# A scan stage on single blocks or on pairs: visits of TensorE, table loads and recurrences

## The chip, the cores and the metric

The kernel runs on one core of a Trainium2 chip. The metric is the device time of one execution in microseconds, lower is better. The core has five engines with queues of their own: TensorE (PE in the profile, its weight loads are PEld), VectorE (DVE), ScalarE (ACT), GpSimd (POOL) and SyncE (SP), which only issues transfers here. They wait for each other by semaphores. Each engine works through its instructions in the order in which they were put into the program.

## The reference

Two layers of a decoder trunk on 256 positions with 2048 channels. The first (state-space scan and attention beside each other) and the closing layer norms are not touched here. The second layer is the one of the change, cut to what matters:

```python
def s5_ssm(u, ...):                      # u: (1, 256, 2048) = 128 groups of 16 channels
    lam_bar = jnp.exp(lam * dt)          # 64 complex states per group
    b_bar = ((lam_bar - 1.0) / lam)[..., None] * (b_re + 1j * b_im)
    bu = jnp.einsum('gnm,blgm->blgn', b_bar, u)      # encode
    hs = scan over l of h = lam_bar * h + bu         # recurrence
    y = jnp.einsum('gmn,blgn->blgm', c_mat, hs).real # decode
    return y + d_skip * u

def s5_mixer(x, ...):
    u, gate = jnp.split(x @ w_in, 2, axis=-1)
    y = gelu(s5_ssm(u, ...))
    ga, gb = jnp.split(y @ w_glu, 2, axis=-1)
    return (ga * sigmoid(gb) * silu(gate)) @ w_out
```

## The kernel before

**The large products.** All weight matrices are streamed once, in units of 512 KB (`raw`, 128 x 1024 floats). For each unit SP loads `raw` (line 227), ACT rounds it to its high part `wh` (L230), and DVE takes the rest `wl` (L232), so that three matmuls of reduced precision give a product of full precision. `split_to` keeps this three units ahead of TensorE, with four buffers each. `wmm` (L297, 24 matmuls of 256 columns a unit) and `xmm` (L276, 12 of 512 columns a unit) are the large matmuls, written to the tiles `main`. `product` runs eight units and after each of them calls `pump`, which hands out the next entries of two lists: `jobs` (work that belongs to the product just done) and `back` (work of a stage in the background, paced by `goal` so that it is spread evenly over the units that are left). So small work is put between the units of the large products. A scheduler then places the instructions of each engine's queue; `tc.issue_after` keeps a job behind a given split in that order.

**The scan stage** is such a background stage. It lies beside the eight products with `wi1` (input projection of the second layer: four products of kind "w" with 256 columns, then four of kind "x" with 512) and the first units of the GLU product. The 128 groups are cut into 16 blocks of 8. For each block `b`, `ssm(b)` gives the steps, and `at(t, f)` files step `f` under the number `t`; all steps, sorted by number, make up `back`. With `t = 2 * b` they are:

- `load` (t - 2): POOL's queue loads the table `wt` (128 x 1792 floats, 896 KB: encode weights, decode weights, and the phase tables `cos` and `sin`) from the scratch `wb`. The tile has four buffers.
- `table` (t - 1): POOL writes the recurrence coefficients `rt`.
- `enc` (t): 16 matmuls of 64 x 64 on the inputs `um` into the tile `enc`. TensorE is used as four quadrants.
- `rec1` (t + 1): DVE turns the result by the phases (four operations of `turned` and two sums, L1159, L1166, L1167).
- `rec2` (t + 2): DVE runs two scans (L1174) into `gt`, turns back (L1161) and combines (L1176, L1177).
- `dec` (t + 4): 24 matmuls of 64 x 64, of which 16 read `gt` (L1190, L1194), into the tile `dec`. It comes in the same step as `enc` of block b + 2, so that one stop of TensorE does both.
- `act` (t + 5): ACT applies GELU into `ys`; after every second block POOL's queue stores it to `yd`.

`u_store` writes the finished columns of `u` to the scratch `ud`; `u_load` (L1115, L1116; four transfers on POOL's queue, for two blocks together) reads them back as `um` in another layout. `y_load` and `y_split` read `yd` back and split it (L1227 on ACT, L1228 on DVE) for the GLU product, which needs the last quarter only in its last two units.

In this text a visit is a stretch in which TensorE leaves the large matmuls for the small ones of `enc` and `dec`.

Of the kernel before, what the change touches and what calls it, by code (L numbers as in the profile page):

```python
# [9 lines left out]
F32 = mybir.dt.float32  # L10
F32R = mybir.dt.float32r
AF = mybir.ActivationFunctionType
# [4 lines left out]
P = 128  # L17
# [145 lines left out]
def trunk(tc, io, out):  # L163
# [4 lines left out]
    def nm(s):  # L168
        count[0] += 1
        return f"{s}_{count[0]}"  # L170

    with ExitStack() as top:
# [917 lines left out]
        with ExitStack() as l1:  # L1090
# [3 lines left out]
            def w1(tag, shape, bufs=2, dt=F32):  # L1094
                return wk.tile(shape, dt, tag=tag, bufs=bufs, name=nm(tag))
# [24 lines left out]
            def at(t, f):  # L1120
                steps.setdefault(t, []).append(f)

            ysd = {}

            def ssm(b):
                j, h, b2 = b // 4, (b // 2) % 2, b % 2
                d = {}
                tiles = [(e, i, i ^ e) for e in range(2) for i in range(2)]

                def load():  # L1130
                    wt = d["w"] = w1("wt", [P, 1792], 4)
                    nc.gpsimd.dma_start(wt, wb[b])
                    ph = wt[:, 1280:1792].rearrange("p (a n) -> p a n", a=2)
                    d["cos"] = ph[:, 0, :].unsqueeze(1).to_broadcast([P, 2, 256])
                    d["sin"] = ph[:, 1, :].unsqueeze(1).to_broadcast([P, 2, 256])

                def table():
                    rt = d["rt"] = w1("rt", [P, 4, 64])
                    G.memset(rt[:, :, 0:1], 0.0)
                    G.tensor_copy(rt[:, :, 1:], rho[:, 4 * b : 4 * b + 4].unsqueeze(2).to_broadcast([P, 4, 63]))  # L1140

                def enc():
                    px = d["x"] = sp.tile([P, 2, 512], F32, tag="enc", name=nm("enc"))
                    wt, u = d["w"], um[b // 2]
                    for q in range(2):
                        for r in range(2):
                            for e, i, at in tiles:
                                a = 2 * q + e
                                T.matmul(px[64 * at : 64 * at + 64, i, r * 128 + q * 64 : r * 128 + q * 64 + 64],  # L1149
                                         wt[64 * i : 64 * i + 64, a * P + 64 * r : a * P + 64 * r + 64],  # L1150
                                         u[64 * i : 64 * i + 64, 4 * b2 + a, :], start=True, stop=True)

                def turned(src):
                    p1, p2 = w1("p1", [P, 2, 256]), w1("p2", [P, 2, 256])
                    for p, t in ((p1, d["cos"]), (p2, d["sin"])):
                        if src is None:
                            t4 = t.rearrange("p r (i n) -> p r i n", i=2)
                            sv = d["x"][:, :, 0:256].rearrange("p i (r n) -> p r i n", r=2)
                            V.tensor_tensor(p.rearrange("p r (i n) -> p r i n", i=2), sv, t4, op=OP.mult)  # L1159
                        else:  # L1160
                            V.tensor_tensor(p, src, t, op=OP.mult)  # L1161
                    return p1, p2

                def rec1():
                    p1, p2 = turned(None)
                    V.tensor_tensor(p1[:, 0], p1[:, 0], p2[:, 1], op=OP.add)  # L1166
                    V.tensor_tensor(p1[:, 1], p1[:, 1], p2[:, 0], op=OP.subtract)  # L1167
                    d["p"] = p1

                def rec2():  # L1170
                    rt = d["rt"].rearrange("p a c -> p (a c)")
                    gt = d["g"] = w1("gt", [P, 2, 256])
                    for r in range(2):
                        V.tensor_tensor_scan(gt[:, r, :], rt, d["p"][:, r, :], 0.0, op0=OP.mult, op1=OP.add)  # L1174
                    p1, p2 = turned(gt)
                    V.tensor_tensor(gt[:, 0], p1[:, 0], p2[:, 1], op=OP.subtract)  # L1176
                    V.scalar_tensor_tensor(gt[:, 1], p1[:, 1], -1.0, p2[:, 0], op0=OP.mult, op1=OP.subtract)  # L1177

                def dec():
                    wt, u, gt = d["w"], um[b // 2], d["g"]  # L1180
                    py = d["y"] = sp.tile([P, 2, 512], F32, tag="dec", name=nm("dec"))
                    for q in range(2):
                        for part in range(3):
                            for e, i, at in tiles:
                                a = 2 * q + e
                                rows = slice(64 * at, 64 * at + 64)
                                o = py[64 * e : 64 * e + 64, at, q * 64 : q * 64 + 64]
                                if part == 0:
                                    rhs = u[rows, 8 + 2 * b2 + q, :] if e else u[rows, 4 * b2 + a, :]
                                    T.matmul(o, wt[rows, 1024 + 64 * a : 1088 + 64 * a], rhs, start=True, stop=False)  # L1190
                                else:
                                    k = 512 + 256 * (part - 1) + 64 * (2 * i + q)
                                    n = 64 * (2 * i + q)
                                    T.matmul(o[:, 1:64], wt[rows, k : k + 64], gt[rows, part - 1, n : n + 63], start=False, stop=part == 2)  # L1194

                def act():
                    if b2 == 0:
                        ysd[0] = w1("ys", [P, 2, 4, 64], 1)
                    ys = ysd[0]
                    A.activation(ys[:, :, 2 * b2 : 2 * b2 + 2, :], d["y"][:, :, 0:128].rearrange("p i (q c) -> p i q c", c=64),  # L1200
                                 AF.Gelu_apprx_tanh)
                    if b2 == 1:
                        dst = yd[j][16 * h : 16 * h + 16].rearrange("(i q e) a c -> e a i q c", i=2, e=2)
                        for i in range(2):
                            nc.gpsimd.dma_start(dst[0, :, i], ys[0:64, i])
                            nc.gpsimd.dma_start(dst[1, :, 1 - i], ys[64:128, i])

                t = 2 * b
                at(t + 5, act)
                at(t + 4, dec)  # L1210
                at(t + 2, rec2)
                at(t + 1, rec1)
                at(t, enc)
                at(t - 1, table)
                at(t - 2, load)

            def y_load(j):
                y5[j] = w1("ut", [P, 4, S], 1)
                nc.gpsimd.dma_start(y5[j], yd[j].rearrange("g a c -> (g a c)").rearrange("(f p t) -> p f t", p=P, t=S))
# [7 lines left out]
                A.activation(y5["h"][:, fs, :], yt, AF.Copy)  # L1227
                V.tensor_tensor(y5["l"][:, fs, :], yt, y5["h"][:, fs, :].bitcast(F32), op=OP.subtract)  # L1228
# [116 lines left out]
```

## Time and profile before

| what | value |
|---|---|
| median of 3 runs | 1352.6 us (1352.0 to 1353.1) |
| the profiled execution | 1355.75 us |
| its span | 1353.9 us |
| granted clock of TensorE | 0.996 |
| DMA, mean over the span | 209 GB/s |
| scan stage, first to last small matmul | 911.6 to 1088.2 us |

The profile is of one execution. Its own time is 3.15 us over the median, and its span is 1.85 us shorter than its own time. In the rows below, a time is the start in us from the span's start, and the length of a matmul is longer than the step to the next one, since they overlap. "<-" in brackets names what ended an engine's idle time. Busy shares are means over stages of different kinds, so the rows of the scan stage count, not those of the page alone.

### The profile page before, as it was taken

How to read it: one execution, taken by the hardware profiler on the slowest of the kernel's cores; microseconds unless marked ns; L12 is line 12 of the kernel's file. 1: busy time of each engine (PE TensorE's matmuls, PEld its weight loads, DVE VectorE, ACT ScalarE, POOL GpSimd, SP SyncE). 2: the span in 40 equal slices, each digit the busy share in tenths (PEclk: the TensorE clock that was granted, in tenths of full speed). 3: DMA queues.
4: the chain of work that ended last, by engine and by line, in shares of the span. 5: the costliest groups of instructions: out<-in, count | busy, mean ns of one | idle time of the engine just before them, and what ended most of it. 6: DMA issues, size and time to landing. Idle time of an engine off the chain costs nothing.

```text
span 1353.9 us, 24904 instructions
## 1 busy us (share of the span) xinstructions
PE 1337.0 (99%) x9839; PEld 1205.5 (89%) x9839; DVE 981.2 (72%) x1560; ACT 673.0 (50%) x870; POOL 364.8 (27%) x648
## 2 busy tenths in 40 slices
PE   9999999999999999999999999999999999999996
PEld 8999999998998998998988888899988888888885
DVE  5767856787687879689787766748889856555556
ACT  5566567764544553554554334334444545444441
POOL 0041000122026528616798500022343100000001
PEclk9999999999999999999999999999999999999998
DMA  8655555545546756856767778497989766666762
GB/s 313 192 171 176 173 171 158 157 143 178 175 135 207 254 163 203 269 160 206 232 206 243 232 232 302 136 300 223 318 275 326 217 211 189 187 196 188 250 214 81
DMA packets 80741, 283.01 MB, mean 209 GB/s; under 512 B 9840, under 2 KB 12528, under 8 KB 80112
## 3 DMA queue, kind: packets, MB, share of 16 engines
q1 hardware_dynamic: 68112, 239.33, 56.2%
q0 software_dynamic: 7328, 30.42, 6.5%
q10 hardware_dynamic: 5184, 11.67, 2.3%
q8 instruction: 77, 1.26, 0.4%
q14 instruction: 40, 0.33, 0.1%
HBM read 260.41 MB, written 20.97 MB: 208 GB/s over the span
## 4 chain that ended last, share of the span: by engine, by line
PE 93%; DVE 4%; DMA 2%; issue 1%; ACT 0%; POOL 0%; SPq 0%; POOLq 0%; ACTq 0%; DVEq 0%
PE main L276 43%; PE main L297 42%; DVE wl L232 1%; PE aux L381 1%; PE aux L812 1%; PE aux L719 1%; PE enc L1149 1%; DMA bc<-in_s5bc 1%; PE dec L1194 1%; PE aux L924 1%; PE aux L892 1%; DMA ud<-ut 0%; PE aux L782 0%; PE dec L1190 0%; PE aux L715 0%
## 5 line engine op out<-in xcount | busy, mean ns | idle before, releaser
L232 DVE TENSOR_TENSOR wl<-raw,wh 128x1024 fp32r<-128x1024 f32 x431 | 538.4, 1251 | 323.4 <-ACT wh L230 317.4
L230 ACT ACTIVATE wh<-raw 128x1024 fp32r<-128x1024 f32 x431 | 455.8, 1059 | 580.3 <-PE main L276 269.2
L297 PE MATMUL main<-A,wh 128*128 128x256 f32 x1408 | 400.7, 285 | 1.3 <-ACT wh L230 1.1
L297 PE MATMUL main<-B,wh 128*128 128x256 f32 x1408 | 398.0, 284 | 0.0
L297 PE MATMUL main<-A,wl 128*128 128x256 f32 x1408 | 394.5, 283 | 0.0
L297 PEld LDWEIGHTS main<-A,wh 128*128 128x128 f32 x1408 | 269.7, 192 | 3.0 <-ACT wh L230 1.3
L297 PEld LDWEIGHTS main<-B,wh 128*128 128x128 f32 x1408 | 269.8, 192 | 0.4
L297 PEld LDWEIGHTS main<-A,wl 128*128 128x128 f32 x1408 | 267.8, 192 | 0.2 <-issue 0.2
L276 PE MATMUL main<-wl,A 128*128 128x512 f32 x512 | 200.5, 392 | 0.5 <-DVE wl L232 0.5
L276 PE MATMUL main<-wh,A 128*128 128x512 f32 x512 | 200.5, 392 | 0.0
L276 PE MATMUL main<-wh,B 128*128 128x512 f32 x512 | 199.9, 390 | 0.0
L276 PE MATMUL main<-wh,C 128*128 128x512 f32 x384 | 150.7, 393 | 0.0
L276 PE MATMUL main<-wh,F 128*128 128x512 f32 x384 | 149.8, 390 | 0.0
L276 PE MATMUL main<-wl,C 128*128 128x512 f32 x384 | 149.7, 390 | 0.0
L276 PEld LDWEIGHTS main<-wl,A 128*128 128x128 f32 x512 | 96.2, 188 | 21.3 <-DVE wl L232 1.8
L276 PEld LDWEIGHTS main<-wh,B 128*128 128x128 f32 x512 | 96.2, 188 | 19.9
L276 PEld LDWEIGHTS main<-wh,A 128*128 128x128 f32 x512 | 96.1, 188 | 19.8 <-issue 0.2
L653 POOL TENSOR_TENSOR c<-c 128x8 f32<-128x8 f32 (+2 forms) x192 | 106.7, 574 | 25.5 <-DMA wb<-c 18.0
L276 PEld LDWEIGHTS main<-wh,F 128*128 128x128 f32 x384 | 72.1, 188 | 15.3
L276 PEld LDWEIGHTS main<-wh,C 128*128 128x128 f32 x384 | 72.1, 188 | 15.1
L276 PEld LDWEIGHTS main<-wl,C 128*128 128x128 f32 x384 | 72.1, 188 | 14.6
L873 POOL TENSOR_TENSOR a<-a,b 64x512 f32<-64x512 f32 x16 | 28.2, 1769 | 169.1 <-DVE b L872 132.1
(279 smaller groups left out, 1651.6 us busy)
## 6 DMA issues: line engine op xcount, KB each, us to landing
raw<-in_wi SPq DMA_DIRECT2D x271, 512.0 KB, 4.0
raw<-in_wo SPq DMA_DIRECT2D x96, 512.0 KB, 4.3
raw<-in_wglu SPq DMA_DIRECT2D x64, 512.0 KB, 3.6
wt<-wb POOLq DMA_DIRECT2D x16, 896.0 KB, 6.9
wb<-ob ACTq DMA_DIRECT2D x16, 512.0 KB, 5.8
bc<-in_s5bc SPq DMA_DIRECT2D x16, 256.0 KB, 4.6
wb<-c POOLq DMA_DIRECT2D x16, 256.0 KB, 3.4
wb<-om ACTq DMA_DIRECT2D x16, 128.0 KB, 4.3
```

The lines of the kernel that those rows point to most:

```text
L230: high = A.activation(wh, raw, AF.Copy)
L232: splits[n] = (loaded[-1], high, V.tensor_tensor(wl, raw, wh.bitcast(F32), op=OP.subtract))
L276: T.matmul(ps[o], l[:, k, sl], r[:, j, :], start=start and i == 0, stop=stop and i == 2)
L297: T.matmul(pv[o // 2][:, o % 2, :], l[:, j, sl], r[:, k, :], start=first and i == 0 and o % 2 == 0, stop=end and i == 2 and o % 2 == 1, sk ...
L381: end = T.transpose(dst[:, i * P : i * P + P], s, ident)
L653: G.tensor_tensor(p[:, :, :, 0:m], cs[:, :, :, 1 : m + 1], cs[:, i, :, n : n + 1].unsqueeze(1).to_broadcast([P, 2, 4, m]), op=OP.mult)
L719: T.matmul(pk[at : at + 64, a * 16 : a * 16 + 16], ev[:, a, 64 * i : 64 * i + 64], cv[:, a, i, :], start=True, stop=True)
L812: T.matmul(yo, xs[:, 0, xc], df[:, i, 0:256], start=True, stop=False)
L873: turns.append(G.tensor_tensor(q[0:64], q[0:64], tm, op=OP.add))
L892: T.matmul(px[:, 128:384], qT[:, h, P:S], kT[:, h, :], start=True, stop=True)
L924: T.matmul(po, v[:, 0, hs], pT[:, i, 0:256], start=True, stop=False)
L1149: T.matmul(px[64 * at : 64 * at + 64, i, r * 128 + q * 64 : r * 128 + q * 64 + 64], wt[64 * i : 64 * i + 64, a * P + 64 * r : a * P + 64 * ...
```

## The change

Steps are made for eight pairs of blocks instead of 16 blocks. One table tile holds both blocks of a pair (two buffers of 2 x 1792), filled by two transfers four steps ahead. `enc` makes the 32 matmuls of a pair, `dec` its 48. The recurrences run over both blocks at once: the products from the tile `enc` stay 512 wide and are four, the sums become 512 wide, the two scans 512, the two products behind them 1024, and the combining of `gt` becomes a step of its own, `rec3`, 512 wide. One GELU serves a pair. `rt`, `p1`, `p2` and `gt` have one buffer instead of two; the GLU stage takes its halves of `gt` and `p1` from them. The inputs `um` are loaded three steps ahead of the encode. The core of the diff:

```diff
-            def ssm(b):
-                j, h, b2 = b // 4, (b // 2) % 2, b % 2
+            def ssm(n):
+                j, h = n // 2, n % 2
...
                 def load():
-                    wt = d["w"] = w1("wt", [P, 1792], 4)
-                    nc.gpsimd.dma_start(wt, wb[b])
...
+                    wt = d["w"] = w1("wt", [P, 2, 1792])
+                    for k in range(2):
+                        nc.gpsimd.dma_start(wt[:, k, :], wb[2 * n + k])
+                    d["cos"], d["sin"] = wt[:, :, 1280:1536], wt[:, :, 1536:1792]

                 def table():
-                    rt = d["rt"] = w1("rt", [P, 4, 64])
+                    rt = d["rt"] = w1("rt", [P, 8, 64], 1)
                     G.memset(rt[:, :, 0:1], 0.0)
-                    G.tensor_copy(rt[:, :, 1:], rho[:, 4 * b : 4 * b + 4].unsqueeze(2).to_broadcast([P, 4, 63]))
+                    G.tensor_copy(rt[:, :, 1:], rho[:, 8 * n : 8 * n + 8].unsqueeze(2).to_broadcast([P, 8, 63]))
...
+                def parts():
+                    return w1("p1", [P, 2, 2, 256], 1), w1("p2", [P, 2, 2, 256], 1)

                 def rec1():
-                    p1, p2 = turned(None)
+                    p1, p2 = parts()
+                    for k in range(2):
+                        for p, t in ((p1, "cos"), (p2, "sin")):
...
+                            V.tensor_tensor(p[:, :, k, :].rearrange("p r (i n) -> p r i n", i=2), sv, t4, op=OP.mult)
                     V.tensor_tensor(p1[:, 0], p1[:, 0], p2[:, 1], op=OP.add)
                     V.tensor_tensor(p1[:, 1], p1[:, 1], p2[:, 0], op=OP.subtract)
                     d["p"] = p1

                 def rec2():
                     rt = d["rt"].rearrange("p a c -> p (a c)")
-                    gt = d["g"] = w1("gt", [P, 2, 256])
+                    gt = d["g"] = w1("gt", [P, 2, 2, 256], 1)
                     for r in range(2):
-                        V.tensor_tensor_scan(gt[:, r, :], rt, d["p"][:, r, :], 0.0, op0=OP.mult, op1=OP.add)
-                    p1, p2 = turned(gt)
+                        V.tensor_tensor_scan(gt[:, r].rearrange("p k n -> p (k n)"), rt, d["p"][:, r].rearrange("p k n -> p (k n)"), 0.0, op0=OP.mult, op1=OP.add)
+                    d["q"] = parts()
+                    for p, t in zip(d["q"], ("cos", "sin")):
+                        V.tensor_tensor(p, gt, d[t].unsqueeze(1).to_broadcast([P, 2, 2, 256]), op=OP.mult)
+
+                def rec3():
+                    gt, (p1, p2) = d["g"], d["q"]
                     V.tensor_tensor(gt[:, 0], p1[:, 0], p2[:, 1], op=OP.subtract)
                     V.scalar_tensor_tensor(gt[:, 1], p1[:, 1], -1.0, p2[:, 0], op0=OP.mult, op1=OP.subtract)
...
-                t = 2 * b
+                t = 4 * n
                 at(t + 5, act)
                 at(t + 4, dec)
+                at(t + 3, rec3)
                 at(t + 2, rec2)
                 at(t + 1, rec1)
                 at(t, enc)
                 at(t - 1, table)
-                at(t - 2, load)
+                at(t - 4, load)
...
-            for b in range(16):
-                ssm(b)
-                if b % 2 == 0:
-                    at(2 * b - 2, lambda b=b: u_load(b // 2))
-                if b % 4 == 3:
-                    at(2 * b + 7, lambda b=b: y_load(b // 4))
-                    at(2 * b + 10, lambda b=b: y_split(b // 4))
+            for n in range(8):
+                ssm(n)
+                at(4 * n - 3, lambda n=n: u_load(n))
+                if n % 2:
+                    at(4 * n + 7, lambda n=n: y_load(n // 2))
+                    at(4 * n + 10, lambda n=n: y_split(n // 2))
...
-                    sb = w1("gt", [P, 2, 256])
-                    t1 = d["t"] = w1("p1", [P, 2, 256])
+                    sb = w1("gt", [P, 2, 2, 256], 1)[:, 0]
+                    t1 = d["t"] = w1("p1", [P, 2, 2, 256], 1)[:, 0]
```

More of the change, by code (lines that the diff above doesn't have):

```diff
@@ L1121, in at @@
                 steps.setdefault(t, []).append(f)
-            ysd = {}
-            def ssm(b):
-                j, h, b2 = b // 4, (b // 2) % 2, b % 2
+            def ssm(n):
+                j, h = n // 2, n % 2
                 d = {}
@@ L1142, in enc @@
                 def enc():
[L1143 to L1162, printed above, removed]
@@ L1164, in rec1 @@
-                def rec1():
-                    p1, p2 = turned(None)
+                    d["x"] = sp.tile([P, 2, 512], F32, tag="enc", name=nm("enc"))
+                    wt, u = d["w"], um[n]
+                    for k in range(2):
+                        px = d["x"][:, :, 256 * k : 256 * k + 256]
+                        for q in range(2):
+                            for r in range(2):
+                                for e, i, at in tiles:
+                                    a = 2 * q + e
+                                    T.matmul(px[64 * at : 64 * at + 64, i, r * 128 + q * 64 : r * 128 + q * 64 + 64],
+                                             wt[64 * i : 64 * i + 64, k, a * P + 64 * r : a * P + 64 * r + 64],
+                                             u[64 * i : 64 * i + 64, 4 * k + a, :], start=True, stop=True)
@@ new lines, in parts @@
+                def parts():
+                    return w1("p1", [P, 2, 2, 256], 1), w1("p2", [P, 2, 2, 256], 1)
+                def rec1():
+                    p1, p2 = parts()
+                    for k in range(2):
+                        for p, t in ((p1, "cos"), (p2, "sin")):
+                            t4 = d[t][:, k, :].unsqueeze(1).to_broadcast([P, 2, 256]).rearrange("p r (i n) -> p r i n", i=2)
+                            sv = d["x"][:, :, 256 * k : 256 * k + 256].rearrange("p i (r n) -> p r i n", r=2)
+                            V.tensor_tensor(p[:, :, k, :].rearrange("p r (i n) -> p r i n", i=2), sv, t4, op=OP.mult)
@@ L1179, in dec @@
                 def dec():
[L1180 to L1194, printed above, removed]
@@ L1196, in act @@
-                def act():
[L1197 to L1206, printed above, removed]
@@ L1208, in ssm @@
-                t = 2 * b
+                    d["y"] = sp.tile([P, 2, 512], F32, tag="dec", name=nm("dec"))
+                    wt, u, gt = d["w"], um[n], d["g"]
+                    for k in range(2):
+                        py = d["y"][:, :, 128 * k : 128 * k + 128]
+                        for q in range(2):
+                            for part in range(3):
+                                for e, i, at in tiles:
+                                    a = 2 * q + e
+                                    rows = slice(64 * at, 64 * at + 64)
+                                    o = py[64 * e : 64 * e + 64, at, q * 64 : q * 64 + 64]
+                                    if part == 0:
+                                        rhs = u[rows, 8 + 2 * k + q, :] if e else u[rows, 4 * k + a, :]
+                                        T.matmul(o, wt[rows, k, 1024 + 64 * a : 1088 + 64 * a], rhs, start=True, stop=False)
+                                    else:
+                                        c = 512 + 256 * (part - 1) + 64 * (2 * i + q)
+                                        m = 64 * (2 * i + q)
+                                        T.matmul(o[:, 1:64], wt[rows, k, c : c + 64], gt[rows, part - 1, k, m : m + 63], start=False, stop=part == 2)
@@ new lines, in act @@
+                def act():
+                    ys = w1("ys", [P, 2, 4, 64], 1)
+                    A.activation(ys, d["y"][:, :, 0:256].rearrange("p i (q c) -> p i q c", c=64), AF.Gelu_apprx_tanh)
+                    dst = yd[j][16 * h : 16 * h + 16].rearrange("(i q e) a c -> e a i q c", i=2, e=2)
+                    for i in range(2):
+                        nc.gpsimd.dma_start(dst[0, :, i], ys[0:64, i])
+                        nc.gpsimd.dma_start(dst[1, :, 1 - i], ys[64:128, i])
+                t = 4 * n
```

3 lines of the change are left out of this document (removed).

## The prediction

> **What bounds the kernel now.** I read the page first: busy shares, then the chain that ended last.
>
> ```profile
> span 1353.9 us, 24904 instructions
> ...
> PE 1337.0 (99%) x9839; PEld 1205.5 (89%) x9839; DVE 981.2 (72%) x1560; ACT 673.0 (50%) x870; POOL 364.8 (27%) x648
> ...
> PE 93%; DVE 4%; DMA 2%; issue 1%; ACT 0%; POOL 0%; SPq 0%; POOLq 0%; ACTq 0%; DVEq 0%
> ```
>
> TensorE holds 93% of the chain and is busy 99% of the span. So only two things can move the end: time that TensorE no longer spends, and time in which it waits. The busy table by stretch narrows this to the scan stage, and the waits of TensorE name its one stall there.
>
> ```profile
> 910.00:950.00 40.00, 38.68 (x506) 37.64 (x505) 30.71 (x44) 15.98 (x19) 11.26 (x21) 1.00 0.79 229
> 950.00:1000.00 50.00, 50.00 (x665) 44.52 (x665) 43.81 (x65) 19.15 (x23) 21.19 (x37) 1.00 0.93 315
> ...
> PE enc L1149 <- DMA um<-ud: 1.3, 1, 1.3
> ```
>
> Columns after the length of the stretch: PE, PEld, DVE, ACT, POOL busy, granted clock, DMA share. From 950 us on TensorE has no gap, at full clock, with DVE busy 43.81 of 50 us. Only at the start does it lose 1.3 us, to the first `um` load. DVE has room, but not much: that decides below.
>
> **Term 1, the visits.** A visit is the train of small matmuls between the large ones. I look at a decode with an encode behind it, and at the last decode, which stands alone, in the timeline of TensorE (start, length, what).
>
> ```profile
> 994.44 0.39 PE L276 MATMUL main<-wl,C 128*128 128x512 f32 x1
> 994.66 0.39 PE L276 MATMUL main<-wh,F 128*128 128x512 f32 x1
> 994.98 0.34 PE L1190 MATMUL dec<-um,wt 64*64 64x64 f32 x8
> 995.15 0.41 PE L1194 MATMUL dec<-gt,wt 64*64 64x63 f32 x16
> 995.38 0.30 PE L1190 MATMUL dec<-um,wt 64*64 64x64 f32 x8
> 995.50 0.41 PE L1194 MATMUL dec<-gt,wt 64*64 64x63 f32 x16
> 995.73 0.66 PE L1149 MATMUL enc<-um,wt 64*64 64x64 f32 x32
> 996.32 0.50 PE L276 MATMUL main<-wh,C 128*128 128x512 f32 x1
> 996.66 0.40 PE L276 MATMUL main<-wl,C 128*128 128x512 f32 x1
> ...
> 1087.20 0.39 PE L276 MATMUL main<-wh,B 128*128 128x512 f32 x1
> ...
> 1088.72 0.40 PE L276 MATMUL main<-wl,A 128*128 128x512 f32 x1
> ```
>
> One large matmul follows another after about 0.227 us (994.44 to 994.66; 0.22 to 0.23 as rounded). From 994.66 to 996.66 are 2.00 us; less two such steps, the 80 small ones cost 1.55 us. The lone decode (the same four decode rows, 48 small ones) takes 1.52 us, less 0.45, so 1.07. The 32 of the encode therefore cost 0.48 us, 15 ns each; 80 of them 1.20, and 0.35 us is left that is paid once per visit, at its two edges. Before there are 19 visits: the first encode in two pieces, the second alone, 14 joint ones, two lone decodes. In the order in which the changed program's instructions stand on TensorE there are 12: one encode, seven joint ones, one decode, and three more because the scheduler cuts the sixth decode into two pieces and the eighth into three. The small matmuls are as many as before. Gain: 7 x 0.35 = 2.4 us. The bounds: at least 1.4, if the encode pieces that now stand inside decodes cost an edge of their own in three visits, at most 2.6.
>
> **Term 2, the first stall.**
>
> ```profile
> 910.02 0.28 PE L297 MATMUL main<-F,wh 128*128 128x256 f32 x1
> 911.62 0.29 PE L1149 MATMUL enc<-um,wt 64*64 64x64 f32 x2 [1.32 <-DMA um<-ud]
> ...
> 905.36 0.72 POOL L1115 DMA_DIRECT2D um<-ud  x1 [5.95 <-DMA ud<-ut]
> ...
> 907.38 0.64 POOL L1116 DMA_DIRECT2D um<-ud  x1
> ```
>
> The changed order puts 34 more large matmuls (0.12 us each in this part) ahead of the first encode: 4.1 us, so TensorE comes to it at 914.2 instead of 910.1. POOL's queue ahead of that load holds the same DMAs as before: four `wt` loads, then the `ud` store. The first `um` load was there at 911.62, 6.3 us after its issue; the fourth, issued at 907.38, is there at about 913.6 by the same time. The stall goes: 1.3 us (bounds 0.5, if the fourth is late by a microsecond, and 1.3). What is late next is nothing in that stretch.
>
> **Term 3, the new wait.** The decode now needs `gt` of both blocks, and `rec3` stands one step ahead of it instead of a step with slack. The recurrences of a block, before:
>
> ```profile
> 930.34 1.23 DVE L232 TENSOR_TENSOR wl<-raw,wh 128x1024 fp32r<-128x1024 f32 x1 [0.72 <-ACT wh L230]
> 931.48 1.27 DVE L1174 TENSOR_TENSOR_SCAN gt<-rt,p 128x256 f32<-128x256 f32 x2
> 932.78 1.49 DVE L1161 TENSOR_TENSOR p<-gt,wt 128x512 f32<-128x512 f32 x2
> 934.19 1.21 DVE L232 TENSOR_TENSOR wl<-raw,wh 128x1024 fp32r<-128x1024 f32 x1
> 935.33 0.41 DVE L1176 TENSOR_TENSOR gt<-p,p 128x256 f32<-128x256 f32 x1
> 935.66 0.41 DVE L1177 SCALAR_TENSOR_TENSOR gt<-p,p 128x256 f32<-128x256 f32 x1
> 936.00 1.27 DVE L1159 TENSOR_TENSOR p<-enc,wt 128x512 f32<-128x512 f32 x2
> 937.30 0.42 DVE L1166 TENSOR_TENSOR p<-p,p 128x256 f32<-128x256 f32 x1
> 937.65 0.42 DVE L1167 TENSOR_TENSOR p<-p,p 128x256 f32<-128x256 f32 x1
> 937.98 1.22 DVE L232 TENSOR_TENSOR wl<-raw,wh 128x1024 fp32r<-128x1024 f32 x1
> ```
>
> From start to start: two scans 1.30, two products 1.41, the two of `gt` 0.67, two products 1.30, two sums 0.68: 5.36 us a block, 10.7 a pair. After: four 512-wide products from PSUM and four 512-wide sums at 0.64; two 512-wide scans, not in this trace, between 0.94 (0.64 and once the 0.30 that 256 more columns cost a plain operation) and 1.27 (two scans), I take 1.2, since a scan takes twice a plain operation; two 1024-wide products between 1.14 (a split, start to start) and 1.41, I take 1.3. Sum 8 x 0.64 + 2.4 + 2.6 = 10.1 us. DVE saves 0.6 us a pair, which is worth nothing by itself.
>
> But all 10.1 us now lie between one encode and its decode. In the built order four or five operations of 1.14 us (splits, and the split of `y`) stand among them, 4.6 to 5.7; and DVE reaches the pair late, as it reached L1159 at 936.00 after an encode that ended at 933.4: 2.5 us, which a split that waits for ACT can make 0 or 5. Together 17.2 to 18.3 us. TensorE's large matmuls between encode and decode are, for the eight pairs, 20.2, 17.3, 19.7, 16.3, 19.1, 19.1, 16.3 and 23.2 us long (168 and 144 of 0.120; 96 with 36 of 0.227; then 72, 84, 84, 72, 102 of 0.227), with 0.5 for edge and first products. So the middle pairs have no margin. Behind the waiting decode on TensorE stand the encode and all large products; DVE's splits run on, three units ahead. Bounds: 0, since DVE has slack left in the stage,
>
> ```profile
> L232 DVE TENSOR_TENSOR wl<-raw,wh 128x1024 fp32r<-128x1024 f32 x67 | 81.7, 1220 | 41.0 <-ACT wh L230 40.9
> ```
>
> (41.0 us idle ahead of the splits between 900 and 1110 us), and 1.3 us on each of seven visits (18.3 less 16.8 is 1.5, which only the shortest windows would show): 9.1 us. I take 0.4 a visit, 2.7 us, by the middle of the two spans.
>
> **What POOL does beside it.** `table` copies the coefficients while DVE multiplies:
>
> ```profile
> 879.82 0.41 POOL L1140 COPY rt<-rho 128x252 f32<-128x252 f32 x1
> ...
> 932.91 0.81 POOL L1140 COPY rt<-rho 128x252 f32<-128x252 f32 x1
> L1161 DVE TENSOR_TENSOR p<-gt,wt x32: 678/693/883, 923.3 to 1081.9; 128x512 f32<-128x512 f32 x32
> ```
>
> Alone the copy took 0.41 us, beside the products 0.81, and a product up to 0.88 instead of 0.69: 0.19 us lost. [...] The doubled copy is a rival below.
>
> **Hidden edits.** Both table loads of a pair are issued behind the decode that frees the tile, a whole pair ahead of their use; so is POOL's queue behind them (stores of `yd`).
>
> ```profile
> raw<-in_wi SPq DMA_DIRECT2D x46, 512.0 KB, 5.3
> wt<-wb POOLq DMA_DIRECT2D x12, 896.0 KB, 6.9
> ```
>
> Two in a row take at most 13.8 us against 16.3 or more; weights that land some microseconds later have three units (8.2 us) of lead. If that cover goes, DVE is late and it is term 3. Single `rt`, `gt`, `p1`, `p2` are freed by DVE or by the decode before their next writer is reached. The last decode stands 18 large matmuls (4.1 us) nearer to the use of its result:
>
> ```profile
> 1105.47 1.23 DVE L1228 TENSOR_TENSOR B<-ut,A 128x1024 fp32r<-128x1024 f32 x1 [0.84 <-ACT A L1227]
> ...
> 1110.72 0.39 PE L276 MATMUL main<-wh,B 128*128 128x512 f32 x1
> ```
>
> The margin was 4.0 us, so this costs 0 to 0.1.
>
> **The sum.** -2.4 - 1.3 + 2.7 = -1.0 us. The profiled execution took 1355.75 us, 3.15 over the median of 1352.6; the difference is taken from that median: 1351.6 us. A measurement of this kernel tells about 0.2% (2.7 us) from no change, so 1349.9 to 1355.3 counts as the same.
>
> **Rivals.** *DVE keeps pace*: `gt` is there at every decode. For it speaks the idle time of DVE; against it the five windows under 19.2 us. -3.7 us: 1348.9. *The pair is late at every visit*: the joint recurrences become the bound, each of seven decodes waiting 1.3 us, 9.1 in all: 1358.0. It is slower than no change in the measurable sense from 0.91 us a visit (6.4 in all). For it speaks that the DVE table shows 43.81 of 50 us; against it that the windows alternate. *POOL's copy shuts DVE out*: at 0.82 us for twice 252 columns in full, 0.63 more than the 0.19 seen, on seven visits 4.4 us on top of my sum: 1356.0. [...] *It doesn't do what it says*: the visits are cut further by waits or keep their edges, and term 1 falls to 1.4 us while a later `um` keeps 0.3 us of the stall: 1352.9.
>
> **Chances.** Forecast 0.47 (its own range 1349.9 to 1354.0, waits of 1.0 to 5.1 us), DVE keeps pace 0.22, late at every visit 0.15, POOL's copy 0.08, not as said 0.08. Faster 0.22; same 0.47 + 0.08 = 0.55; slower 0.15 + 0.08 = 0.23. The range from 1348.7 (the fast case with term 1 at its 2.6) to 1358.0 (the slow case) leaves out under 2 in 10.
>
> **What would show it.** 12 visits on TensorE with 0.35 us of edges each; no wait for `um`; waits of the decode for DVE (L1178 or L1177) of 2.7 us in all, on the middle pairs; scans of about 1.2 us and 1024-wide products of 1.3. Waits under 1 us or over 5 us, or a new wait of the large products for a split, prove me wrong.

## The result and the profile after

| kernel | median us | lowest to highest | runs |
|---|---|---|---|
| before | 1352.66 | 1352.0 to 1353.18 | 6 |
| changed | 1362.43 | 1360.17 to 1363.63 | 6 |

The ratio is 1.007, with a 95% interval of 1.0057 to 1.0083: the change costs 9.8 us. The forecast was 1351.6, and the range ended at 1358.0.

The page of the changed kernel hardly shows it (span, busy shares, the chain that ended last):

```profile
span 1358.3 us, 24771 instructions
...
PE 1335.9 (98%) x9839; PEld 1206.2 (89%) x9839; DVE 975.7 (72%) x1496; ACT 672.3 (49%) x862; POOL 385.4 (28%) x632
...
PE 92%; DVE 2%; DMA 2%; issue 1%; ACT 1%; POOL 0%; SPq 0%; POOLq 0%; ACTq 0%; DVEq 0%
```

This execution took 1360.17 us, the fastest of the six. A second profile of the same kernel, of an execution of 1361.89 us, is nearer to the median; from here on its rows are used. The waits of TensorE from 860 to 1115 us (waiting instruction, what released it, sum, times, longest):

```profile
PE enc L1148 <- issue: 2.5, 1, 2.5
PE enc L1148 <- DMA wt<-wb: 2.0, 1, 2.0
PE main L297 <- DVE F L1048: 1.3, 1, 1.3
PE dec L1197 <- DVE gt L1177: 1.0, 1, 1.0
PE main L297 <- issue: 1.0, 1, 1.0
PE dec L1197 <- DVE gt L1178: 0.5, 2, 0.3
```

The wait for `um` is gone, and the wait for `F` near 873 us stands in the kernel before too. New are three things: stalls that the profile gives to nobody ("issue", 3.5 us), a wait for the tables `wt` (2.0), and one for `gt` (1.5). And TensorE loses clock behind them. The busy table of six microseconds after the waits for `wt` and `gt` (length, then busy times, granted clock, DMA share, GB/s):

```profile
1001.00:1007.00 6.00, 5.30 (x142) 4.84 (x143) 3.26 (x4) 0.00 (x0) 2.93 (x5) 0.72 0.83 274
1007.00:1012.00 5.00, 5.00 (x24) 4.14 (x23) 2.26 (x3) 3.33 (x4) 0.90 (x3) 1.00 1.05 228
```

The clock record of this trace has half clock for 3.4 us from 1002.4 on, which is the 0.72 over 6 us: 1.7 us lost.

**What happens at the "issue" stalls.** The larger one is in the timeline of TensorE (start, length, what):

```profile
1068.41 0.30 PE L1193 MATMUL dec<-um,wt 64*64 64x64 f32 x8
1068.53 0.41 PE L1197 MATMUL dec<-gt,wt 64*64 64x63 f32 x16
1068.76 0.88 PE L1148 MATMUL enc<-um,wt 64*64 64x64 f32 x46
1072.14 0.34 PE L1148 MATMUL enc<-um,wt 64*64 64x64 f32 x8 [2.50 <-issue]
1072.42 0.50 PE L276 MATMUL main<-wh,C 128*128 128x512 f32 x1
```

It stops in the middle of an encode, between matmuls that read the same tiles, which speaks against a wait for data (the second round of experiments tests it). The transfers of 1.6 us in that pause, by DMA queue (packets, MB, share of the 16 engines):

```profile
q1 hardware_dynamic: 113, 0.41, 80.3%
q8 instruction: 1, 0.02, 3.6%
```

One packet of a queue named "instruction" lands in the pause, after none in the 3.4 us before it. On the page this queue has:

```profile
q8 instruction: 77, 1.26, 0.4%
```

77 packets of 16 KB. TensorE has 2 x 9839 recorded instructions (matmuls and weight loads), which is 255.6 for each packet; so the packets are taken here for TensorE's program, in blocks of 256 instructions. Counted by TensorE's records in the trace, the two "issue" stalls of the changed kernel come after matmul 6982 and after matmul 8515, in both profiles; the distance, 1533 matmuls, is twelve blocks of 128 but for 3, and from the one to the other twelve packets land in the first profile. There TensorE goes on at 939.21 and 1070.49 us, 1.43 and 1.54 us after the packet has landed (937.78 and 1068.95). A joint visit (decode and encode together) is 160 matmul records now, 320 instructions, where it was 80 records and 160 instructions. So it can start on one block, use up the next and stand in front of the one after it within 2.4 us (an estimate, 160 x 15 ns).

At the other ends of blocks TensorE lost nothing that shows: over the whole span of the first profile it has no "issue" wait of 0.3 us or more but these two (1.6 and 0.9 us), with 77 packets. So it is the dense trains that can cost: one crossing cost up to 3.7 us in the runs below.

**What makes `wt` late.** POOL's queue in the second profile, 20 us ahead of that visit:

```profile
972.36 7.16 POOL L1137 COPY rt<-rho 128x504 f32<-128x504 f32 x1
979.46 0.77 POOL L1105 DMA_DIRECT2D ud<-ut  x1
986.48 0.75 POOL L1219 DMA_DIRECT2D ut<-yd  x1 [6.25 <-DMA ud<-ut]
...
990.90 1.10 POOL L1131 DMA_DIRECT2D wt<-wb  x2
```

The copy of 504 coefficients took 7.16 us; where it was not held, it took 0.62 (995.93 us in the first profile). DVE over the same time:

```profile
972.10 1.20 DVE L232 TENSOR_TENSOR wl<-raw,wh 128x1024 fp32r<-128x1024 f32 x1
973.22 2.36 DVE L1173 TENSOR_TENSOR p<-gt,wt 128x1024 f32<-128x1024 f32 x2
975.49 1.22 DVE L232 TENSOR_TENSOR wl<-raw,wh 128x1024 fp32r<-128x1024 f32 x1
976.63 0.69 DVE L1177 TENSOR_TENSOR gt<-p,p 128x512 f32<-128x512 f32 x1
977.23 0.69 DVE L1178 SCALAR_TENSOR_TENSOR gt<-p,p 128x512 f32<-128x512 f32 x1
977.83 1.22 DVE L232 TENSOR_TENSOR wl<-raw,wh 128x1024 fp32r<-128x1024 f32 x1
979.79 1.23 DVE L232 TENSOR_TENSOR wl<-raw,wh 128x1024 fp32r<-128x1024 f32 x1 [0.74 <-ACT wh L230]
```

DVE runs seven instructions from 972.10 on without a gap until 979.05, with all inputs in SBUF, and the copy ends 0.46 us later, in DVE's first idle time. (The copy of 8.29 us at 1042.20 ends 0.46 us behind such a run too, though DVE goes on there with products on `enc`, which lies in PSUM; that the place of the inputs decides was not shown.) DVE loses nothing beside this copy (its two products take 2.36 us together, start to end; in the first profile, beside the same copy, 2.35, at a median of 1.22 for one over the stage); POOL loses 6.5 us. Behind it in POOL's queue stand the store of `ud`, then the load of `y` into the same tile `ut`, which waits 6.25 us for that store, then `um` and the tables: issued at 990.90; TensorE comes to them at 998.0 and can go on with them at 999.9. The late `y` holds its split on DVE (3.2 us idle), and the pair's products queue behind that split: this is the wait for `gt`.

### The profile page after: what moved, and what is told of

Same layout as the page of the kernel before. It is cut to its first block, busy times and chain, and to the rows that moved or that the text cites. A ratio compares the mean times of both kernels' runs of the same rounds, so it can differ in the third digit from the quotient of the medians.

```text
span 1358.3 us, 24771 instructions
## 1 busy us (share of the span) xinstructions
PE 1335.9 (98%) x9839; PEld 1206.2 (89%) x9839; DVE 975.7 (72%) x1496; ACT 672.3 (49%) x862; POOL 385.4 (28%) x632
## 4 chain that ended last, share of the span: by engine, by line
PE 92%; DVE 2%; DMA 2%; issue 1%; ACT 1%; POOL 0%; SPq 0%; POOLq 0%; ACTq 0%; DVEq 0%
PE main L297 43%; PE main L276 41%; PE aux L381 1%; PE aux L812 1%; PE aux L719 1%; DMA yd<-ys 1%; DMA raw<-in_wi 1%; PE dec L1197 1%; DMA ut<-yd 1%; PE aux L924 1%; PE aux L715 1%; PE aux L892 1%; PE enc L1148 1%; DVE wl L232 0%; PE aux L782 0%
```

## The experiments

The ratios below are to the kernel before as run on the same chip beside them (medians of 1352.6 to 1353.6 us). The rounds ran on different chips, so medians of two rounds are set against each other only by their distances from these. In the edits `[...]` stands for an index left out, and `unused` for a table that nobody reads by then.

### First round: whose copy is it

**Copy by DVE.**

```diff
-G.tensor_copy(rt[:, :, 1:], rho[...])
+V.tensor_copy(rt[:, :, 1:], rho[...])
```

> The changed kernel, with the copy of the recurrence coefficients (504 columns a pair) made by DVE instead of POOL; nothing else. Theory (POOL's copy was held back beside DVE's products, 0.6 us to 8.3 us, and the table loads and stores behind it in POOL's queue came late): the encode's wait for wt at about 997 us, the wait of the GELU's successors for y and the stalls between 930 and 1095 us go. The gains of the visits (2.4) and of the first stall (1.3) stay, DVE pays about 0.6 us a pair: 1349 to 1352 us. Rival, burst (the two table loads in a row are too much for the DMA engines, whenever they are issued): 1361 to 1363, the encode still waits 2 us or more for wt. Rival, joint recurrences (the decode waits because both blocks' recurrences lie in front of it): 1363 or more, the waits for gt grow over the 1.5 us seen.

1357.9 us, ratio 1.0027 (1.0015 to 1.0040). The waits for `wt` and `gt` are gone, so neither the burst of two loads nor the joint recurrences make TensorE wait. But the time is 6 us above the theory. What is left are the "issue" stalls, now the only waits in the stage (waits of TensorE, 900 to 1130 us):

```profile
PE enc L1148 <- issue: 3.7, 1, 3.7
PE main L297 <- issue: 1.4, 1, 1.4
```

They stand after matmul 6982 and 8515 again, and 3.4 us of half clock follow the larger one (the large matmuls behind it stand 0.42 us apart instead of 0.227; the granted clock is 0.98 from 1000 to 1100 us).

**Two narrower copies.**

```diff
+for k in range(2):
+    G.tensor_copy(rt[:, 4*k : 4*k+4, 1:], rho[...])
```

> The changed kernel, with POOL's copy of 504 columns cut into two copies of 252, as wide as those before the change. Theory, if POOL gets in between two instructions of DVE and the length of the copy is what matters: each copy takes 0.4 to 1.2 us as before the change, POOL's queue is late by 2.4 us at most, 1350 to 1354 us. If DVE's dense run keeps POOL out whatever the copy's length: one of the two copies still takes 4 to 8 us, 1360 to 1363. Rivals burst and joint recurrences: 1361 to 1363 too, with copies that may be short.

1361.9 us, ratio 1.0046 (1.0031 to 1.0061). Pairs of copies still took 7.10, 7.28, 8.09 and 8.42 us: the width of the copy is not what keeps POOL out.

**Two buffers for the coefficients.**

```diff
-rt = w1("rt", [P, 8, 64], 1)
+rt = w1("rt", [P, 8, 64], 1) if n % 2 == 0 else ct[:, 384:896]
```

> The changed kernel, with two buffers for the coefficients rt as before the change (the second in a constant table that is no longer used by then). The copy no longer waits for the scans of the pair before, so it starts when POOL comes to it, some 6 us earlier. Theory: the queue behind it is no longer late, even if the copy is stretched: 1350 to 1355 us, no wait for wt. Rivals burst and joint recurrences: 1361 to 1363, as without this edit.

1366.0 us, ratio 1.0083 (1.0065 to 1.0102). A miss: the copy did not come earlier (974.2 us, 7.16 us long), since POOL still waits there until the scans are through. It says nothing on the theory; why it is some 3 us slower than the changed kernel was not followed.

**POOL kept busy, first try.**

```diff
+V.tensor_copy(rt[:, :, 1:], rho[...])
+if n:
+    for i in range(17):
+        G.memset(unused, 0.0)
```

> The kernel with DVE's copy, and with POOL kept busy for about 7 us (17 memsets of 128 x 384 on an unused table) at each of seven pairs in the place where the copy stood. DVE and TensorE are given nothing to do for it. Theory (a late POOL queue costs the time): 1357 to 1364 us, with waits of the encode for wt and late y loads. Rivals (DVE, or the burst): the time of the kernel with DVE's copy, within 1 us.

1358.0 us. Inconclusive: all 119 memsets ran between 810 and 867 us, ahead of the stage. It is a second measurement of DVE's copy.

### Second round: the blocks of instructions

From the places of the two stalls, the other block ends can be counted off, and so which visits would be hit if TensorE's program were some instructions longer ahead of the stage. All runs of this round have DVE's copy.

**Program moved by 26 matmul records.**

```diff
-warm(WARM1)
+warm(WARM1, 13)   # 13 more matmuls, 64 x 64, on zeros
```

> DVE's copy as before, and 13 matmuls of 64 x 64 on a tile of zeros added to the warm-up ahead of the stage (26 matmul records; they fill time in which TensorE waits for DVE). They move every later instruction of TensorE against the blocks of 256 instructions in which its program is fetched. Theory (fetch: a visit of 320 instructions uses up a block before the next one is there; the stalls after matmul 6982 and 8515 are that): the two stalls go, at most 1.1 us of stalls remain in the stage, 1348.5 to 1351.5 us, ratio about 0.998. Rival (the two stalls are waits for data, tables or um, that the profile does not name): both stalls stay at the visits near 935 and 1062 us, 1357 to 1359 us.

1351.6 us, ratio 0.9990 (0.9981 to 0.9999). 13 useless matmuls take 5.5 us off the kernel with DVE's copy (4.3 us above the kernel before there, 1.25 below it here). In its profile the second stall is away, and one row is left:

```profile
PE enc L1152 <- issue: 1.0, 1, 1.0
```

It stands after matmul 6982 again, which is now 26 records further up the program: inside the encode, not behind it.

**Program moved by 86 records.**

```diff
+warm(WARM1, 43)
```

> As the run before, but with 43 small matmuls (86 records) in the warm-up. Theory (fetch): the visits near 934 and 1061 us no longer stall, but those near 955, 1019 and 1040 us do, since a block of instructions now begins 20 to 41 records into them: 4 to 9 us of stalls, 1357 to 1363 us. Rival (data): stalls at the visits near 935 and 1062 us as with no small matmuls, 1357 to 1359 us.

1358.6 us, ratio 1.0042 (1.0028 to 1.0055). The visits near 934 and 1061 run through, others stall (rows of TensorE's timeline):

```profile
958.14 0.28 PE L297 MATMUL main<-C,wh 128*128 128x256 f32 x1 [0.88 <-issue]
...
1000.55 0.45 PE L1152 MATMUL enc<-um,wt 64*64 64x64 f32 x13 [0.65 <-issue]
...
1025.97 0.27 PE L1152 MATMUL enc<-um,wt 64*64 64x64 f32 x1 [3.21 <-issue]
```

Two of the three visits named (955, 1019) and one not named (997, in place of 1040); 4.7 us in all, as expected. Counted as above, they come after matmuls 7365, 7876 and 8132, which are 3, 7 and 9 blocks of 128 behind 6982, but for 1 or 2. So with the two places above, five places of stalls in three programs of different length lie on one grid of blocks. The page of this run has 78 packets of the queue "instruction" instead of 77. A cause in the data would not follow the count of instructions.

**Decode as a visit of its own.**

```diff
-at(t + 5, act)
-at(t + 4, dec)
-at(t - 4, load)
+at(t + 6, act)
+at(t + 5, dec)
+at(t - 3, load)
```

> DVE's copy, and the decode one step later, so that a pair's decode is a visit of its own (24 to 80 large matmuls behind the next encode; table loads are issued one step later as well). 128 or 192 instructions of TensorE in a row instead of 320. Theory (fetch): no stall over 1 us without a named cause in the stage; seven visits more cost 7 x 0.35 = 2.4 us, the first stall of 1.3 stays away: 1351 to 1353 us. Rival (data, or DVE): the stalls stay, 1358 us or more by the visits' 2.4.

1351.8 us, ratio 0.9990 (0.9981 to 0.9999), and no wait of TensorE in the stage at all. In that profile 192 instructions in a row do not outrun the fetch.

**POOL kept busy, second try.**

```diff
+V.tensor_copy(rt[:, :, 1:], rho[...])
+for i in range(64):
+    G.memset(rt[:, :, 0:1], 0.0)
```

> DVE's copy, and POOL kept busy for about 7 us a pair by 64 memsets of the zero columns of the coefficient tile, which start only when DVE has copied (in the run before of this kind the memsets were placed ahead of the stage and delayed nothing in it). Theory (a late POOL queue cost the part that DVE's copy won): the wait of the encode for wt near 997 us comes back, 1360 to 1366 us. [...]

1367.6 us, ratio 1.0103 (1.0087 to 1.0118), but by another way than meant: the scans read the tile that the memsets write, and DVE waited for them (waits of DVE):

```profile
DVE gt L1172 <- POOL rt L1139: 8.4, 2, 7.9
```

TensorE waited 7.4 us for `gt` and 0.2 for `wt`. It tells nothing on the queue alone.

### Third round: the parts by themselves

**POOL's copy back, needed by nobody.**

```diff
+V.tensor_copy(rt[:, :, 1:], rho[...])
+G.tensor_copy(unused, rt[:, :, 1:])
```

> The kernel with DVE's copy (1357.9 us), and POOL copying the coefficients on to a table that nobody reads, in the place where its copy stood: POOL's work is back, but no result depends on it except the next pair's DVE copy. Theory (POOL's copy is held back beside DVE's run and the loads and stores behind it come late): copies of up to 7 or 8 us again, wt or y late near 997 us, TensorE waits there 2 us or more and gets half its clock for some microseconds; 1361 to 1365 us. Rival (what DVE's copy won was the direct wait of the scan for POOL's result): the copy may be long, but the time stays at 1357 to 1359 us.

1358.0 us, ratio 1.0036 (1.0023 to 1.0048). Copies of up to 5.0 us, no wait for `wt` or `y`: the rival's time. But near 971 us this copy stood behind the store of `ud`, not ahead of it, and the fetch stalls were still there (3.7 us after matmul 8515), which may hide such a cost.

**The changed kernel with the program moved by 26 records.**

```diff
-warm(WARM1)
+warm(WARM1, 13)   # POOL's copy kept
```

> The changed kernel itself, POOL's copy kept, with the 13 small matmuls in the warm-up: the instruction stalls are taken away alone. Theory (two causes that add: fetch some 6 us, POOL's copy some 4 to 6): 1354 to 1358 us, no stall near 1069, the wait for wt near 997 us stays. Rival (one of the two is all of it, the other goes with it): 1351 to 1353 us, or still over 1360.

1352.2 us (1351.2 to 1356.5), ratio 1.000 (0.999 to 1.001): 10.2 us less than the changed kernel, by 13 matmuls that compute nothing. That is not the theory of two causes that add, but the rival: with one cause most of the other goes too. The copies are as long as ever (7.16 and 8.29 us); three of ten runs took 1353.6 to 1356.5, among them the profiled one, the slowest, whose waits from 860 to 1115 us are:

```profile
PE dec L1201 <- DVE gt L1181: 1.8, 1, 1.8
PE enc L1152 <- issue: 1.3, 1, 1.3
PE enc L1152 <- DMA wt<-wb: 0.6, 1, 0.6
PE dec L1201 <- DVE gt L1182: 0.3, 1, 0.3
```

The stall after matmul 6982 is left here too (1.3 us).

**The kernel before with the same 13 matmuls.**

```diff
-warm(WARM1)
+warm(WARM1, 13)
```

> The kernel before, with the 13 small matmuls in the warm-up. Theory (they act by moving the blocks of instructions, and visits of 160 instructions never use up a block): no difference, ratio 0.999 to 1.001. Rival (they win by filling the wait of TensorE near 873 us): 1 us or more faster.

1351.65 us, ratio 0.9991 (0.9982 to 1.0000), so 1.0 us of the gain by the 13 matmuls is not the fetch. In its profile TensorE does not wait for DVE near 873 us (1.3 us before): the rival's reason. There was no "issue" stall to take away.

**First decode apart as well.**

```diff
-at(t + 5, act)
-at(t + 4, dec)
-at(t - 4, load)
+at(t + 5 + (n == 0), act)
+at(t + 4 + (n == 0), dec)   # with DVE's copy and the 13 matmuls
+at(t - 4 + (n == 2), load)
```

> DVE's copy, the 13 small matmuls, and the first pair's decode one step later, as a visit of its own (the load of the third pair's tables with it). Theory (fetch): the stall of 1.2 us left in the first joint visit goes, one edge of 0.35 us comes; 1349.5 to 1351 us, no stall over 0.5 us in the stage. Rival (what is left is not fetch): 1351.5 us or more.

1350.6 us, ratio 0.9979 (0.9970 to 0.9987), no stall of 0.5 us in the stage. It beats the kernel before by 2.0 us, and the kernel before with the 13 matmuls by 1.1: that is what the change itself is worth once its own stalls are out.

### Fourth round: what POOL's copy costs

**The same with the copy on POOL.**

```diff
-V.tensor_copy(rt[:, :, 1:], rho[...])
+G.tensor_copy(rt[:, :, 1:], rho[...])
```

> The changed kernel with POOL's copy kept, the 13 small matmuls and the first pair's decode as a visit of its own: no fetch stalls. If POOL's copy costs by itself (late tables and late y at the visit near 997 us): 1352 to 1356 us, a wait for wt or gt of 1 us or more there, longer than the same kernel with DVE's copy (1350.6) by 2 us or more. If it costs only where a fetch stall comes on top: 1350 to 1351.5 us.

1354.9 us (1350.8 to 1356.7), ratio 1.0007 (0.9998 to 1.0016): 3.6 us over the kernel with DVE's copy by the distances from the kernel before (1.5 above, 2.0 below), though single runs are as fast as that. In this order of work POOL's copy costs by itself. Its profile can't show how: it is of the fastest run (1350.8), in which the copy took 7.16 us at the same place, the tables were issued at 986.53, and TensorE waited 0.7 us, for `gt`. And without the decode set apart POOL's copies cost 0.8 us (0.4 below the kernel before against 1.25 below).

**Four useless copies a pair.**

```diff
+V.tensor_copy(rt[:, :, 1:], rho[...])
+for i in range(4):
+    G.tensor_copy(unused, rt[:, :, 1:])
```

> The kernel with DVE's copy and four useless copies of POOL a pair, of which at least the first is held back beside DVE's run; POOL's queue is late by 6 to 9 us where one such copy made it late by up to 5. If the lateness of POOL's queue is the way: waits for wt or y of 1 us or more, 1360 to 1365 us. If it is not: 1357 to 1359 us as with one copy.

1358.0 us, ratio 1.0036 (1.0024 to 1.0048): no more than with one, and within 0.5 us of none (4.7 above the kernel before against 4.3). POOL's queue was held for up to 7.0 us near 1039, and TensorE did not wait there.

**The changed kernel again**, for the second profile used above.

> The changed kernel once more, unchanged, for a second profile. If fetch is the larger part: stalls without a named releaser behind matmul 6982 and 8515 again, the second of 2 to 4 us, with half the clock behind it; 1360 to 1364 us. If the first profile told it right: the waits for wt and gt are larger than those stalls.

1362.0 us. Stalls behind the same two matmuls, the second of 2.5 us. The half clock, though, stood behind the waits for `wt` and `gt`, and these sum to as much as the stalls.

**One copy of eight given to DVE.**

```diff
+(V if n == 3 else G).tensor_copy(rt[:, :, 1:], rho[...])
```

> As after_best, but the coefficients of one pair of the eight, the fourth, are copied by DVE: the copy that took 7.2 us near 970 us, ahead of the store of ud. The other seven stay on POOL, the one of 8.3 us among them. If that copy's lateness, handed on by POOL's queue (store of ud, load of y, um, tables), is the cost: the store stands some 7 us earlier, the wait at the visit near 994 us goes, 1350 to 1351.5 us in nearly all runs. If the other long copies cost as well, or DVE's run is what suffers: 1353 to 1355.5 us.

1351.1 us (1350.0 to 1351.9), ratio 0.9985 (0.9976 to 0.9994). The other seven copies stay on POOL. POOL's queue at the same place:

```profile
969.08 0.77 POOL L1109 DMA_DIRECT2D ud<-ut  x1 [0.40 <-ACT ut L1108]
976.06 0.75 POOL L1223 DMA_DIRECT2D ut<-yd  x1 [6.21 <-DMA ud<-ut]
...
980.73 1.10 POOL L1135 DMA_DIRECT2D wt<-wb  x2
```

The tables are issued 10.2 us earlier by the clock (6.4 us earlier, counted from the memset ahead of the copy), and TensorE's one named wait in the stage is 0.3 us for `gt`. So it is this copy, ahead of the store of `ud`, and not DVE's run (it lost nothing beside this copy) nor POOL's lateness as such: two other copies are still held for 7.03 and 8.29 us, and useless copies behind that store left the time within 1.1 us. This one cost 3.6 us (2.05 below the kernel before against 1.5 above). That it cost so by the tables and `y` is argued from the second profile of the changed kernel, not seen in a slow run of this pair.

**The kernel before, two more profiles.**

> The kernel before, unchanged, for a second profile. If the wait for the first um load belongs to the kernel: 1.0 to 1.5 us again near 911 us. If it belonged to that execution: under 0.5 us, and a time near 1352.6.

> The kernel before, unchanged, for a third profile; the same two expectations.

1354.1 and 1352.3 us. Both profiles have a single wait of TensorE from 860 to 1115 us, and it is not for `um`:

```profile
PE main L297 <- DVE F L1048: 1.3, 1, 1.3
```

## Why the prediction was wrong, point by point

**What bounds the kernel: right, and incomplete.** TensorE sets the end. But the two ways in which it can lose time were looked for in its waits for other engines and transfers. That an engine can wait for its own program was on no list, because no row of before shows it: with 160 instructions a visit none of its three profiles has such a stall in the stage.

**Term 1, the visits: right, and the step that failed stands in it.** 12 visits came as said. A joint visit in the first profile of the changed kernel:

```profile
1024.44 0.39 PE L276 MATMUL main<-wh,F 128*128 128x512 f32 x1
1024.76 0.34 PE L1193 MATMUL dec<-um,wt 64*64 64x64 f32 x8
...
1027.30 0.50 PE L276 MATMUL main<-wh,C 128*128 128x512 f32 x1
1027.63 0.39 PE L276 MATMUL main<-wl,C 128*128 128x512 f32 x1
```

3.19 us from 1024.44 to 1027.63, less two steps 2.74, against 2 x 1.55 before: 0.36 saved, 0.35 forecast. What failed is "15 ns each" carried from 80 records to 160 as if the rate had no end. It had one here, a block of 256 instructions by the count above: in or behind each of two visits of the changed kernel the next block was not there in time (1.6 and 0.9 us in the first profile, 1.0 and 2.5 in the second). The stalls alone were 2.5 and 3.5 us in its two profiles, as much as the seven edges gained (7 x 0.36 = 2.5) or more, and moving the program took 10.2 us off.

**Term 2, the first stall: not the kernel's.** It was 1.3 us in the profile of before and nowhere in two others. That profile lay 3.15 us over the median, and a stretch of half clock (0.51 granted from 874.9 to 878.3 us) was in it too; its mean granted clock over the whole span was 0.996, that of the other two 0.997 and 0.998. Taking a gain read in such a profile off the median was the mistake.

**Term 3, the wait for `gt`: priced well, forecast too high.** Groups of DVE in the stage, first profile (count, busy, mean ns):

```profile
L1173 DVE TENSOR_TENSOR p<-gt,wt 128x1024 f32<-128x1024 f32 x16 | 19.9, 1285 | 0.1
L1161 DVE TENSOR_TENSOR p<-enc,wt 128x512 f32<-128x512 f32 x32 | 19.8, 681 | 0.6 <-PE enc L1148 0.6
L1170 DVE TENSOR_TENSOR_SCAN gt<-rt,p 128x512 f32<-128x512 f32 x16 | 18.8, 1208 | 0.0
```

Scans of 1.21 (1.2 taken), products of 1.29 (1.3 taken). The wait was 1.5 us instead of 2.7, at one visit mostly, and came from the late `y`; with DVE's copy there is none. The rival "DVE keeps pace" had this part right. (Seven times the 0.4 taken is 2.8, where the sum has 2.7.)

**What POOL does beside it: right pair, wrong victim.** The rows were read for what DVE loses (0.19 us). Beside the three longest copies of the changed kernel (6.90, 7.16 and 8.29 us) DVE loses nothing and POOL 6 to 8 us; where POOL gets in earlier, one or two of DVE's instructions take 0.2 to 0.66 us longer, about 2 us over the whole stage (first profile). In the second profile POOL was held beside seven of DVE's instructions in a row (972.36 to 979.05), through their boundaries. The step "so is POOL's queue behind them" in the hidden edits then fell: the two loads serve TensorE 9.0 us after their issue, inside the 13.8 allowed, but are issued 10 us behind the decode that frees the tile.

**The sum.** Forecast -1.0, measured +9.8. By the distances from the kernel before, the move of the program alone takes 10.2 off the changed kernel, 1.0 of it by filling the wait near 873 us; DVE's copy alone takes 5.5 off; both together 11.0. So they overlap, and a sum of single prices does not exist here. After both, and with the first decode apart, the change is worth 1.1 us, where six visits fewer at 0.36 would be 2.2; the other half was not traced.

**Still open.** Why moving the program also spares most runs the waits near 997 us, though the copy there is as long, was not settled; nor why POOL's copies cost 3.6 us with the first decode apart and 0.8 without. Nor was why POOL's copy got in at the first boundary of DVE's run before the change (0.81 us, at most 1.21), and only after four to eight of DVE's instructions in four of the eight copies after it; the narrower copies rule out its width alone.

## What to carry to other kernels

Count the instructions that an engine executes in a dense train, and compare them with the blocks in which its program arrives (320 against 256 here): two short trains were cheaper than one long one (ratio 0.9990 against 1.0027 with DVE's copy), and useless instructions elsewhere moved a stall away or brought one (13 matmuls took 10.2 us off the changed kernel, 43 brought a stall of 3.2 us). Where one engine is slower beside another (POOL's copy here, 0.62 to 8.29 us), price both sides, and follow the queue behind the one that loses. Before taking a wait in a profile for a gain, see that the profiled execution lies at the median.

## What the runs showed of the hardware that was not expected

- The queue "instruction" moved 77 packets of 16 KB, one for 255.6 of TensorE's recorded instructions. In or behind dense trains of 320 instructions the next block was late at up to three visits, by 0.4 us (with four useless copies a pair) to 3.7 us (with DVE's copy), and in the first profile of the changed kernel TensorE went on 1.43 and 1.54 us after the packet had landed; in the profile with trains of 128 and 192 instructions there was no such stall.
- Some waits of TensorE were followed by 3.4 us of half clock, a cost of 1.7 us that no wait shows: those for `wt` and `gt` in the first profile of the changed kernel (2.4 and 1.2 us; 0.50 granted from 1001.5 to 1004.9) and in the second (0.72 from 1001 to 1007), and the stall of 3.7 us with DVE's copy. It was not a fixed rule: the stall of 2.5 us in the second profile went without (1.00 from 1060 to 1080), and the wait of 1.3 us near 873 us had it in the first profile of the kernel before (0.51 from 874.9 to 878.3).
- A POOL copy of 0.62 us was held for up to 8.29 us beside an unbroken run of DVE instructions.
